# PSUM banks in a two-layer hybrid block: five for the projections and three for the mixers, in place of six and two

## The chip, the cores and the metric

The kernel runs on one core of one Trainium2 chip. The metric is the device time of one execution in microseconds (us). A core has a matrix engine, TensorE (PE in the profile, with its weight loader shown apart as PEld), a vector engine (DVE), a scalar engine (ACT), a general engine (POOL) and a queue that issues transfers (SP). Matmuls write into PSUM, which here is eight banks of 128 partitions by 512 fp32 values; the other engines read the results from there.

## The reference, cut to what matters

Two layers over 1024 tokens and a model width of 2048. Each layer normalises and modulates the input, projects it with one wide matrix, sends the parts of the projection through three mixers, gates them, and projects back:

```python
def hybrid_layer(x, c, positions, ...):
    shift, scale, gate = jnp.split(jax.nn.silu(c) @ w_mod + b_mod, 3, axis=-1)
    h = rms_norm(x, g_pre) * (1.0 + scale[:, None, :]) + shift[:, None, :]
    proj = h @ w_in
    a_q, a_k, a_v, s_u, s_v, c_q, c_k, c_v, c_g, z = jnp.split(proj, offsets, axis=-1)
    a_q, a_k = partial_rope(a_q, positions), partial_rope(a_k, positions)
    y_a = sliding_window_attention(a_q, a_k, a_v, swa_sinks)         # 16 heads, 4 kv heads, window 128
    y_b = chunked_spatial_gating(gelu(s_u), gelu(s_v), sg_w, sg_b, sg_ln_g, sg_ln_b)
    log_alpha = log_sigmoid(c_g @ gla_w_gate_up + gla_b_gate) / 16.0
    y_c = rms_norm(gated_linear_attention(c_q, c_k, c_v, log_alpha), gla_norm_g)
    y = jnp.concatenate([y_a, y_b, y_c], axis=-1) * jax.nn.silu(z)
    return x + gate[:, None, :] * rms_norm(y @ w_out, g_post)

def reference(x, c, positions, w_mod, ...):
    for l in range(2):
        x = hybrid_layer(x, c, positions, w_mod[l], ...)
    return x
```

## The kernel before, in words

The tokens are split into two halves of 512, and a layer runs over one half after the other, so there are four phases (l, h). A phase has an input part (`in_phase`) and an output part (`out_phase`).

**Projections.** Both parts are made of groups. A group (`group`, L394) computes 512 columns by 512 tokens as four results of 128x512, each in a PSUM bank of its own; one group of 256 columns (`ck`) uses two banks. It loops over the 2048 rows of the weight in eight chunks of two k of 128. For each k and each result m it issues three matmuls (fp32 split into a high and a low part: L381 to L383 where the weight is stationary, L389 to L391 where the activations are). `w_take` hands it a split chunk: L367 on ACT makes the high part, L368 on DVE the low one. The whole kernel has 11,904 such projection matmuls. The groups of an input part come in this order: keys and gla queries (`kcq`), gla keys (`ck`), values, `q0`, `cv`, `q1`, and then `zc`, `sv`, `su`, `zb`, `za0`, `za1`.

**Evacuation.** When its last k is done, a group's four banks are read, and the next group can use a bank once its reader has ended. The reader depends on the group: `evac` is an ACT copy (L768, or L770 with a scale); `silu2` a tanh on ACT and a product on DVE (L427, L428); in the output part ACT takes the sum of squares (L993) and DVE the product with the gate (L995). `gelu2`, used for `sv` and `su`, copies the bank first (L435, ACT) and then works on two tiles of the pool `t2`: square (L436, ACT), L437 and L438 (DVE), tanh (L439, ACT), and the last product (L440, DVE). `t2` has four tiles, so two results are in work at a time.

**Mixers.** Beside the projections run lanes: generators for attention (`att`), gated linear attention (`gla`), spatial gating (`sg`), the modulation (`mod`) and the end of an output part (`fin`). After every three matmuls of a group `tick()` lets a lane go on when its delay has passed, so mixer matmuls stand between projection matmuls in the program. Their results go into the second PSUM pool by `mxt()`. The ones that matter here: attention scores (L491) take two banks at a time and are read by L498 or L500 (ACT) and L501 (DVE); the transposes of the probabilities (L533) wait for their normalisation (L520) and are read by L536; the gla score blocks (L634, L650, L656) are read by `put` (L621, DVE, eight small copies); the transposes of the next phase's input (`h_fill`, L287) by L289. L263 is the sum of squares of the second half's input rows (`x_stats`), L224 a step of the modulation.

**What sets the order.** The program names work in the order above; a planner in the framework then sets the order on each engine from the program's order, priorities (`urgent()` lifts by 300, `evac` by 600) and the pools: an instruction that needs a tile is placed when the planner sees the tile free. The sizes of the two PSUM pools therefore set both which bank a group waits for and the order of instructions on the engines.

The first group, in the start of the kernel, has six results; its banks are taken at once at L1060:

```python
        psk = [pjt() for _ in range(6)]
```

Of the kernel before, what the change touches and what calls it, by code (L numbers as in the profile page):

```python
# [18 lines left out]
PSUM = bass.MemoryType.PSUM  # L19
# [20 lines left out]
def hybrid_kernel(ctx: ExitStack, tc: tile.TileContext, a, y_out):  # L40
# [6 lines left out]
    whl_p = ctx.enter_context(tc.tile_pool(name="whl", bufs=3))  # L47
    t2_p = ctx.enter_context(tc.tile_pool(name="t2", bufs=4))
    sm = ctx.enter_context(tc.tile_pool(name="sm", bufs=2))
    pj = ctx.enter_context(tc.tile_pool(name="pj", bufs=6, space=PSUM))  # L50
    mx = ctx.enter_context(tc.tile_pool(name="mx", bufs=2, space=PSUM))
    pools = {}

    V, S, G, PE = nc.vector, nc.scalar, nc.gpsimd, nc.tensor
# [1 line left out]
    def load(out, in_):  # L56
        nc.sync.dma_start(out=out, in_=in_)

    def urgent():
        return tc.high_priority(offset=PRIO)  # L60
# [35 lines left out]
    def t2(shape=(P, 512), dt=F32):  # L96
        return t2_p.tile(list(shape), dt, tag="t2", name="t2")
# [7 lines left out]
    def mxt():  # L105
        return mx.tile([P, 512], F32, tag="mx", name="mx")

    def pjt():
        return pj.tile([P, 512], F32, tag="pj", name="pj")
# [13 lines left out]
    def rsqrt(out, src, n, pool=sm):  # L123

        i = pool.tile([P, n], I32, tag="rq_i", name="rq_i")
        V.tensor_scalar(i, src.bitcast(I32), 1, None, ALU.logical_shift_right)
        V.tensor_scalar(i, i, -1.0, 1597463007.0, ALU.mult, ALU.add)
        yv = i.bitcast(F32)
        for it in range(3):
            w = pool.tile([P, n], F32, tag="rq_w", name="rq_w")  # L130
            V.tensor_tensor(w, yv, yv, ALU.mult)
            V.scalar_tensor_tensor(w, w, -0.5, src, ALU.mult, ALU.mult)
            dst = out if it == 2 else yv
            V.scalar_tensor_tensor(dst, w, 1.5, yv, ALU.add, ALU.mult)
            yv = dst
# [51 lines left out]
    def mod_columns(l, c, acc, partials):  # L187

        tp = mxt()
        if partials == P:  # L190
            for s in range(4):
                PE.matmul(tp[:, s:s + 1], lhsT=acc[:, s * P:(s + 1) * P], rhs=ones[:, 0:1], start=True, stop=True)
            m = tp[:, 0:4]
        else:
            for s in range(4):
                PE.transpose(tp[:, s * P:(s + 1) * P], acc[:, s * P:(s + 1) * P], ident)
            m = col(4, "mod_m")
            V.tensor_reduce(m, tp.rearrange("p (s r i) -> p s r i", s=4, i=32)[:, :, :, 0], AX.X, ALU.add)
        m = m.rearrange("p (k s) -> p k s", k=2)
        j = slice(2 * c, 2 * c + 2)  # L200
        V.tensor_tensor(bcol[l][:, j], m[:, :, 0], mb[l][:, 0, j], ALU.add)
        t = col(2, "mod_t")
        V.tensor_tensor(t, m[:, :, 1], mb[l][:, 1, j], ALU.add)
        V.scalar_tensor_tensor(acol[l][:, j], t, 1.0, gpc[l][:, j], ALU.add, ALU.mult)
# [147 lines left out]
    def w_load():  # L352
        if wat[0] < len(wsrc):
            src, cols = wsrc[wat[0]]
            wat[0] += 1
            if deep and wat[0] % 2:
                raw = pools["pt"].tile([P, KC, cols], F32, tag="PT", name="wraw2")
            else:
                raw = wraw_p.tile([P, KC, cols], F32, tag="wraw", name="wraw")
            load(raw, src)  # L360
            raws.append(raw)

    def w_split():
        if raws:
            raw = raws.popleft()
            hl = whl_p.tile([P, 2] + list(raw.shape[1:]), F32R, tag="whl", name="whl")
            S.copy(hl[:, 0], raw)  # L367
            V.tensor_tensor(hl[:, 1], raw, hl[:, 0].bitcast(F32), ALU.subtract)  # L368
            ready.append(hl)
            w_load()  # L370
# [6 lines left out]
    def mm_f(ps, hl, k2, m, slot, k):  # L377

        c = slice(m * P, (m + 1) * P)
        whi, wlo = hl[:, 0, k2, c], hl[:, 1, k2, c]  # L380
        PE.matmul(ps, lhsT=whi, rhs=slot[:, 0], start=(k == 0), stop=False)  # L381
        PE.matmul(ps, lhsT=whi, rhs=slot[:, 1], start=False, stop=False)  # L382
        PE.matmul(ps, lhsT=wlo, rhs=slot[:, 0], start=False, stop=(k == NK - 1))  # L383
# [630 lines left out]
    with tc.tile_pool(name="start", bufs=1) as st:  # L1014

        load(mb[0], a["b_mod_col"][0])
        load(gpc[0], a["g_pre"][0])
        xq = [act_p.tile([P, 2, H], F32, tag="act", name="xq") for _ in range(8)]
        for c in range(8):
            load(xq[c], a["x_f"][0, 2 * c:2 * c + 2].rearrange("j p t -> p j t"))  # L1020
        scb = st.tile([P, NK, 32], F32, name="scb")
        V.tensor_copy(scb, sc.unsqueeze(2).broadcast_to([P, NK, 32]))
        ws, raw_q, hl_q = deque(), deque(), deque()

        def first_load(k):
            if k < NK:
                r = wraw_p.tile([P, 1, 768], F32, tag="wraw", name="wraw")
                load(r[:, 0, 0:512], a["w_in"][0, 0, :, k])
                load(r[:, 0, 512:], a["w_ck"][0, :, k])
                raw_q.append(r)  # L1030

        def first_split():
            r = raw_q.popleft()
            hl = whl_p.tile([P, 2, 1, 768], F32R, tag="whl", name="whl")
            S.copy(hl[:, 0], r)  # L1035
            V.tensor_tensor(hl[:, 1], r, hl[:, 0].bitcast(F32), ALU.subtract)
            hl_q.append(hl)

        def mod_load(c, part):
            if c < 8:  # L1040
                w = st.tile([P, 8, 512], F32, name="wm0", bufs=3)
                load(w, a["w_mod"][0, c, :, 8 * part:8 * part + 8])
                ws.append(w)
        mod_load(0, 0)
        mod_load(0, 1)
        mod_load(1, 0)
        first_load(0)


        sums = mxt()  # L1050
        for c in range(8):
            sq = st.tile([P, 2, H], F32, name="sq", bufs=2)
            S.activation(sq, xq[c], AF.Square)
            s2 = st.tile([P, H], F32, name="s2", bufs=2)
            V.tensor_tensor(s2, sq[:, 0], sq[:, 1], ALU.add)
            PE.matmul(sums, lhsT=ones, rhs=s2, start=(c == 0), stop=(c == 7))
        r0 = st.tile([P, H], F32, name="r0")
        V.tensor_scalar(r0, sums, 1.0 / D, EPS, ALU.mult, ALU.add)
        rsqrt(r0, r0, H, st)
        psk = [pjt() for _ in range(6)]  # L1060

        def project(k):
            first_split()
            if k >= NK - 2:
                w_load()
            hl = hl_q.popleft()
            for m in range(6):
                mm_f(psk[m], hl, 0, m, slots[k], k)

        def mod_products(mps, part):  # L1070

            w = ws.popleft()
            for kk in range(8):
                k = 8 * part + kk
                r = 32 * (k % 4)
                PE.matmul(mps[r:r + 32, :], lhsT=scb[:, k], rhs=w[:, kk], start=(k < 4), stop=(k >= 12))  # L1076

        def fill(c, mps):
            acc = st.tile([P, 512], F32, name="mod_acc", bufs=2)
            S.copy(acc, mps)  # L1080
            mod_columns(0, c, acc, 4)
            for j in range(2):
                k = 2 * c + j
                xt, b = t2(), bcol[0][:, k:k + 1]
                V.scalar_tensor_tensor(xt, xq[c][:, j], acol[0][:, k:k + 1], r0, ALU.mult, ALU.mult)
                s = act_p.tile([P, 2, 512], F32R, tag="act", name="act")
                S.activation(s[:, 0], xt, AF.Identity, bias=b)
                V.scalar_tensor_tensor(s[:, 1], xt, b, s[:, 0].bitcast(F32), ALU.add, ALU.subtract)
                slots.append(s)

        for c in range(8):
            if c:
                mod_load(c, 1)
                first_load(2 * c - 1)
            mps = mxt()
            mod_products(mps, 0)
            if c:
                project(2 * c - 2)  # L1100
                mod_load(c + 1, 0)
                first_load(2 * c)
            mod_products(mps, 1)
            with urgent():
                fill(c, mps)
            if c:
                project(2 * c - 1)
            if c == 5:
                for _ in rope_tables(0):
                    pass  # L1110
        first_load(NK - 1)
        project(NK - 2)
        project(NK - 1)
        w_split()
        w_split()
# [147 lines left out]
```

## Time and profile before

| | |
|---|---|
| median of 3 runs | 3080.06 us (3077.67 to 3081.16) |
| profiled execution | 3080.16 us |
| its span | 3078.4 us |
| mean granted TensorE clock | 0.993 |
| TensorE busy | 3005.8 us, 98% |
| weight loader busy | 2445.1 us, 79% |
| DVE busy | 1840.0 us, 60% |
| ACT busy | 1198.9 us, 39% |
| DMA, mean | 152 GB/s |

The span is the time from the first to the last instruction of the profiled execution. Its own time is 1.8 us longer and is the one to compare with the runs. A row of the timeline gives the start and the length of an instruction, and in brackets how long its engine sat idle before it and what ended that. Matmuls overlap: a bar is longer than the distance from one start to the next.

### The profile page before, as it was taken

Reading aid. Unit: us, or ns where it says so; the run is one execution under the profiler, and the core shown is the slowest. Engines: PE = TensorE matmul, PEld = TensorE weight load, DVE = VectorE, ACT = ScalarE, POOL = GpSimd, SP = SyncE. Lnnn points to the kernel's source line nnn. Section 1 sums busy time; section 2 is a strip of 40 time slices with the busy share of each in tenths; the row PEclk is TensorE's granted clock in tenths of the full one; section 3 lists DMA queues with packets and bytes.
Section 4 is the critical chain, followed back from the end, with each engine's and each line's share of the span. In section 5 each row is a group of like instructions: output and inputs, shape, how many; then the busy total and the mean of one; then the engine's idle time right before and its main releaser. Section 6 shows DMA issues by size and latency. Waiting matters only on the chain.

```text
span 3078.4 us, 44118 instructions
## 1 busy us (share of the span) xinstructions
PE 3005.8 (98%) x17298; PEld 2445.1 (79%) x17298; DVE 1840.0 (60%) x2956; ACT 1198.9 (39%) x2367; POOL 24.9 (1%) x68
## 2 busy tenths in 40 slices
PE   7999999999998999999999999999999999999998
PEld 4678777888887887888888887888888888788886
DVE  4678777563867877744364766644346476663425
ACT  3355345232434544323244544423233444342323
POOL 0000000000000000000000000000000000000000
PEclk9999999999999999999999999999999999999999
DMA  9745457575775445644455223334446322343535
GB/s 393 260 138 154 141 171 219 156 232 161 236 226 161 124 131 175 184 130 137 120 168 154 86 72 99 114 118 143 117 129 192 102 80 84 111 131 106 167 103 168
DMA packets 216448, 468.96 MB, mean 152 GB/s; under 512 B 21008, under 2 KB 74672, under 8 KB 214192
## 3 DMA queue, kind: packets, MB, share of 16 engines
q1 hardware_dynamic: 216240, 466.15, 48.9%
q8 instruction: 135, 2.21, 0.3%
q14 instruction: 73, 0.60, 0.1%
HBM read 429.37 MB, written 36.70 MB: 151 GB/s over the span
## 4 chain that ended last, share of the span: by engine, by line
PE 81%; DMA 7%; DVE 7%; ACT 3%; issue 2%; SPq 0%; DVEq 0%; ACTq 0%
PE pj L381 13%; PE pj L382 12%; PE pj L383 12%; PE pj L389 12%; PE pj L391 12%; PE pj L390 12%; DMA wm<-in_w_mod_dram 4%; PE mx L491 2%; PE mx L547 1%; DVE whl L368 1%; DMA t<-in_gla_norm_g_dram 1%; DVE ma L224 1%; DMA wm<-in_x_dram 1%; PE mx L1076 1%; PE mx L533 1%
## 5 line engine op out<-in xcount | busy, mean ns | idle before, releaser
L368 DVE TENSOR_TENSOR whl<-wraw,whl 128x1024 fp32r<-128x1024 f32 (+2 forms) x504 | 587.2, 1165 | 706.1 <-ACT whl L367 705.2
L367 ACT CAST whl<-wraw 128x1024 fp32r<-128x1024 f32 (+2 forms) x504 | 506.0, 1004 | 1128.1 <-PE pj L391 576.1
L389 PE MATMUL pj<-whl,act 128*128 128x512 f32 (+1 forms) x2048 | 784.1, 383 | 0.0
L390 PE MATMUL pj<-whl,act 128*128 128x512 f32 (+1 forms) x2048 | 776.8, 379 | 0.0
L391 PE MATMUL pj<-whl,act 128*128 128x512 f32 (+1 forms) x2048 | 776.6, 379 | 0.0
L381 PE MATMUL pj<-act,whl 128*128 128x512 f32 x1920 | 763.4, 398 | 9.3 <-ACT whl L1035 3.6
L383 PE MATMUL pj<-act,whl 128*128 128x512 f32 x1920 | 749.2, 391 | 3.7 <-DVE whl L368 3.7
L382 PE MATMUL pj<-act,whl 128*128 128x512 f32 x1920 | 751.5, 391 | 0.0
L381 PEld LDWEIGHTS pj<-act,whl 128*128 128x128 f32 x1920 | 361.5, 188 | 109.3 <-issue 23.0
L391 PEld LDWEIGHTS pj<-whl,act 128*128 128x128 f32 x2048 | 385.7, 188 | 72.4 <-issue 0.7
L389 PEld LDWEIGHTS pj<-whl,act 128*128 128x128 f32 x2048 | 386.2, 189 | 69.2 <-issue 2.1
L390 PEld LDWEIGHTS pj<-whl,act 128*128 128x128 f32 x2048 | 386.1, 189 | 67.4 <-issue 1.2
L383 PEld LDWEIGHTS pj<-act,whl 128*128 128x128 f32 x1920 | 361.9, 188 | 82.1 <-DVE whl L368 5.0
L382 PEld LDWEIGHTS pj<-act,whl 128*128 128x128 f32 x1920 | 362.1, 189 | 71.7 <-issue 1.1
L224 DVE SCALAR_TENSOR_TENSOR ma<-wm,sc,ma 128x512 f32<-128x512 f32 x240 | 179.5, 748 | 117.0 <-DMA wm<-in_w_mod_dram 115.3
L517 ACT ACTIVATE M<-M,at_nm 128x128 f32<-128x128 f32 x256 | 99.7, 391 | 50.0 <-DVE at_nm L509 50.0
L536 DVE TENSOR_TENSOR PT<-mx,amask 128x1024 f32<-128x1024 f32 x64 | 77.3, 1218 | 15.7 <-PE mx L533 15.5
L501 DVE COPY_PREDICATED M<-pmask,mx 128x256 f32<-128x256 uint8 x128 | 50.6, 441 | 54.4 <-ACT M L500 42.9
L491 PE MATMUL mx<-kh,qs 128*128 128x256 f32 (+1 forms) x256 | 67.7, 297 | 7.7 <-DVE hold L621 7.5
L491 PE MATMUL mx<-kl,qs 128*128 128x256 f32 (+1 forms) x256 | 66.1, 286 | 0.0
L547 PEld LDWEIGHTS mx<-PT,v 128*64 128x64 f32 x960 | 53.1, 137 | 15.1 <-issue 7.1
L500 ACT COPY M<-mx 128x256 f32<-128x256 f32 x96 | 31.7, 374 | 84.9 <-PE mx L491 84.8
(224 smaller groups left out, 2331.7 us busy)
## 6 DMA issues: line engine op xcount, KB each, us to landing
wraw<-in_w_in_dram SPq DMA_DIRECT2D x312, 512.0 KB, 3.6
wraw<-in_w_out_dram SPq DMA_DIRECT2D x136, 512.0 KB, 3.6
wm<-in_w_mod_dram SPq DMA_DIRECT2D x256, 256.0 KB, 3.3
wm<-in_w_mod_dram SPq DMA_DIRECT2D x16, 2048.0 KB, 13.5
y<-at SPq DMA_DIRECT2D x64, 256.0 KB, 2.8
q<-y SPq DMA_DIRECT2D x64, 256.0 KB, 3.3
q<-x SPq DMA_DIRECT2D x36, 256.0 KB, 2.7
wraw<-in_w_vcg_dram SPq DMA_DIRECT2D x32, 272.0 KB, 2.9
```

What stands on the lines that cost most here:

```text
L224: V.scalar_tensor_tensor(acc, ws[k], sc[:, k:k + 1], acc, ALU.mult, ALU.add)
L367: S.copy(hl[:, 0], raw)
L368: V.tensor_tensor(hl[:, 1], raw, hl[:, 0].bitcast(F32), ALU.subtract)
L381: PE.matmul(ps, lhsT=whi, rhs=slot[:, 0], start=(k == 0), stop=False)
L382: PE.matmul(ps, lhsT=whi, rhs=slot[:, 1], start=False, stop=False)
L383: PE.matmul(ps, lhsT=wlo, rhs=slot[:, 0], start=False, stop=(k == NK - 1))
L389: PE.matmul(ps, lhsT=slot[:, 0, c], rhs=whi, start=(k == 0), stop=False)
L390: PE.matmul(ps, lhsT=slot[:, 0, c], rhs=wlo, start=False, stop=False)
L391: PE.matmul(ps, lhsT=slot[:, 1, c], rhs=whi, start=False, stop=(k == NK - 1))
L491: PE.matmul(sps[p][:, b, k0:], lhsT=qs[:, p, n * P:(n + 1) * P], rhs=keys[2 * j + p][:, n * P + k0:n * P + 256], start=(part == 0), stop=( ...
L517: S.activation(Mf[:, k], Mf[:, k], AF.Exp, bias=nm[:, k:k + 1], scale=0.125, accum_out=den[:, k:k + 1])
L547: PE.matmul(yp[64 * p:64 * p + 64, n * P:(n + 1) * P], lhsT=vv[:, g * 64:g * 64 + 64], rhs=pts[p][:, w, n], start=(w == 0), stop=(w == 1 o ...
```

## The change

Pool `pj`, from which the groups take their banks, has five in place of six, and pool `mx`, from which the mixers take theirs, three in place of two; the sum stays eight. The first group takes one of its six banks from `mx`.

```diff
-    pj = ctx.enter_context(tc.tile_pool(name="pj", bufs=6, space=PSUM))
-    mx = ctx.enter_context(tc.tile_pool(name="mx", bufs=2, space=PSUM))
+    pj = ctx.enter_context(tc.tile_pool(name="pj", bufs=5, space=PSUM))
+    mx = ctx.enter_context(tc.tile_pool(name="mx", bufs=3, space=PSUM))
...
-        psk = [pjt() for _ in range(6)]
+        psk = [mxt()] + [pjt() for _ in range(5)]
```

The change moves instructions. The first place is TensorE at the change from group `su` to group `zb` in the second phase (1274 us in the trace before). pj_11271 to pj_11274 are the four banks of the new group, m=0 to m=3; act_6759 is the activation of its k=0, act_6780 that of k=1. Before:

```order
L382 MATMUL pj_11273<-act_6759,whl_11168 128x512
L383 MATMUL pj_11273<-act_6759,whl_11168 128x512
L381 MATMUL pj_11274<-act_6759,whl_11168 128x512
L382 MATMUL pj_11274<-act_6759,whl_11168 128x512
L383 MATMUL pj_11274<-act_6759,whl_11168 128x512
L381 MATMUL pj_11271<-act_6780,whl_11168 128x512
L382 MATMUL pj_11271<-act_6780,whl_11168 128x512
```

And in the changed kernel at the same place:

```order
L383 MATMUL pj_11273<-act_6759,whl_11168 128x512
L381 MATMUL pj_11271<-act_6780,whl_11168 128x512
L382 MATMUL pj_11271<-act_6780,whl_11168 128x512
L383 MATMUL pj_11271<-act_6780,whl_11168 128x512
L381 MATMUL pj_11272<-act_6780,whl_11168 128x512
L382 MATMUL pj_11272<-act_6780,whl_11168 128x512
L383 MATMUL pj_11272<-act_6780,whl_11168 128x512
L381 MATMUL pj_11273<-act_6780,whl_11168 128x512
L382 MATMUL pj_11273<-act_6780,whl_11168 128x512
L383 MATMUL pj_11273<-act_6780,whl_11168 128x512
L381 MATMUL pj_11274<-act_6759,whl_11168 128x512
```

The three matmuls of m=3 for k=0 now stand behind the nine of m=0 to m=2 for k=1. The same holds at the other changes of group behind a gelu.

The second place is ACT at the gelu near 501 us. pj_4233 and pj_4234 are the first two banks that are read; the rows of L263 belong to the sum of squares of the input rows. Before:

```order
L263 ACTIVATE junk_4885,xss_4499<-wm_4883 128x128
L263 ACTIVATE junk_4887,xss_4499<-wm_4883 128x128
L263 ACTIVATE junk_4889,xss_4499<-wm_4883 128x128
L263 ACTIVATE junk_4891,xss_4499<-wm_4883 128x128
L263 ACTIVATE junk_4912,xss_4499<-wm_4910 128x128
L263 ACTIVATE junk_4914,xss_4499<-wm_4910 128x128
L435 COPY t2_4661<-pj_4233 128x512
L263 ACTIVATE junk_4916,xss_4499<-wm_4910 128x128
L436 ACTIVATE t2_4662<-t2_4661 128x512
L435 COPY t2_4670<-pj_4234 128x512
```

In the changed kernel:

```order
L263 ACTIVATE junk_4885,xss_4499<-wm_4883 128x128
L263 ACTIVATE junk_4887,xss_4499<-wm_4883 128x128
L435 COPY t2_4661<-pj_4233 128x512
L263 ACTIVATE junk_4889,xss_4499<-wm_4883 128x128
L436 ACTIVATE t2_4662<-t2_4661 128x512
L435 COPY t2_4670<-pj_4234 128x512
L263 ACTIVATE junk_4891,xss_4499<-wm_4883 128x128
L367 CAST whl_4700<-wraw_4565 128x1024
```

Four of the six L263 ahead of the first copy now stand behind it, three of them between the second copy and the third.

The third place is TensorE near 371 us, where the transposes of the probabilities (L533) stand between projection matmuls. mx_3465 and mx_3484 are two mixer banks; act_639 and act_644 are the activations of two successive k. Before:

```order
L389 MATMUL pj_3252<-whl_3361,act_639 128x512
L390 MATMUL pj_3252<-whl_3361,act_639 128x512
L391 MATMUL pj_3252<-whl_3361,act_639 128x512
L389 MATMUL pj_3249<-whl_3361,act_644 128x512
L390 MATMUL pj_3249<-whl_3361,act_644 128x512
L391 MATMUL pj_3249<-whl_3361,act_644 128x512
L389 MATMUL pj_3250<-whl_3361,act_644 128x512
L390 MATMUL pj_3250<-whl_3361,act_644 128x512
L391 MATMUL pj_3250<-whl_3361,act_644 128x512
L533 MATMUL mx_3465<-ident_81,M_3315 128x128 x4
L533 MATMUL mx_3484<-ident_81,M_3315 128x128 x4
```

In the changed kernel:

```order
L389 MATMUL pj_3252<-whl_3361,act_639 128x512
L533 MATMUL mx_3465<-ident_81,M_3315 128x128 x4
L390 MATMUL pj_3252<-whl_3361,act_639 128x512
L391 MATMUL pj_3252<-whl_3361,act_639 128x512
L533 MATMUL mx_3484<-ident_81,M_3315 128x128 x4
L389 MATMUL pj_3249<-whl_3361,act_644 128x512
```

The first four transposes stand eight projection matmuls earlier, the second four six.

## Rows read from the trace of the kernel before

**Rows 1.** The page's busy shares: microseconds, share of the span, instructions

```profile
PE 3005.8 (98%) x17298; PEld 2445.1 (79%) x17298; DVE 1840.0 (60%) x2956; ACT 1198.9 (39%) x2367; POOL 24.9 (1%) x68
```

**Rows 2.** Timeline near 1592: start, length, engine line operation, [idle before <-releaser]

```profile
1591.69 2.15 DVE L995 TENSOR_TENSOR hold<-pj,gp 128x512 f32<-128x512 f32 x3
1592.81 0.39 PE L381 MATMUL pj<-act,whl 128*128 128x512 f32 x1
1593.49 0.39 PE L381 MATMUL pj<-act,whl 128*128 128x512 f32 x1
```

**Rows 3.** Tile view, mixer tiles: TensorE idle (us, times) until the named one

```profile
  DVE hold L621: 9.1, 4
  DVE PT L536: 2.7, 3
```

**Rows 4.** Waits of the weight loader: us in total, times, longest

```profile
PEld mx L491 <- issue: 9.9, 8, 6.6
PEld mx L634 <- issue: 5.0, 10, 1.9
PEld mx L491 <- DVE M L501: 3.1, 10, 0.5
PEld mx L634 <- DVE PT L536: 2.1, 3, 1.3
```

**Rows 5.** Timeline near 991: gla copies and the next scores

```profile
989.45 2.03 DVE L621 COPY_PREDICATED hold<-gmask,mx 32x128 f32<-32x128 uint8 x8
991.41 0.55 PE L491 MATMUL mx<-kh,qs 128*128 128x256 f32 x1 [6.18 <-DVE hold L621]
```

**Rows 6.** Timeline near 1274: gelu, the next group's matmuls

```profile
1273.90 0.39 PE L381 MATMUL pj<-act,whl 128*128 128x512 f32 x1
1279.99 0.59 ACT L435 COPY t<-pj 128x512 f32<-128x512 f32 x1 [1.11 <-DVE hold L440]
```

**Rows 7.** Timeline near 453: gelu of the first phase

```profile
453.27 0.39 PE L381 MATMUL pj<-act,whl 128*128 128x512 f32 x1
458.04 0.60 PE L533 MATMUL mx<-ident,M 128*128 128x128 f32 x4
458.21 0.59 ACT L435 COPY t<-pj 128x512 f32<-128x512 f32 x1
```

**Rows 8.** Timeline near 1967: gelu in layer 2

```profile
1967.38 0.39 PE L381 MATMUL pj<-act,whl 128*128 128x512 f32 x1
1971.39 0.59 ACT L435 COPY t<-pj 128x512 f32<-128x512 f32 x1 [1.11 <-DVE hold L440]
```

**Rows 9.** Timeline near 501: gelu behind the row statistics

```profile
504.07 0.31 ACT L263 ACTIVATE junk<-wm 128x128 bf16<-128x128 f32 x1
504.38 0.57 ACT L435 COPY t<-pj 128x512 f32<-128x512 f32 x1
505.00 0.79 PE L381 MATMUL pj<-act,whl 128*128 128x512 f32 x1 [2.91 <-ACT t L435]
510.18 0.58 ACT L435 COPY t<-pj 128x512 f32<-128x512 f32 x1 [0.24 <-DVE hold L440]
```

**Rows 10.** Timeline near 867: the group of two banks

```profile
867.62 0.39 PE L381 MATMUL pj<-act,whl 128*128 128x512 f32 x1
870.78 1.05 ACT L768 COPY t<-pj 128x512 f32<-128x512 f32 x2
873.37 0.50 PE L381 MATMUL pj<-act,whl 128*128 128x512 f32 x1 [0.83 <-ACT whl L367]
875.73 0.50 PE L383 MATMUL pj<-act,whl 128*128 128x512 f32 x1 [1.62 <-DVE whl L368]
```

**Rows 11.** Timeline near 821: group behind an output group

```profile
823.65 0.50 PE L381 MATMUL pj<-act,whl 128*128 128x512 f32 x1 [1.32 <-DVE hold L995]
```

**Rows 12.** Timeline near 371: transposes of the probabilities

```profile
371.04 1.07 PE L533 MATMUL mx<-ident,M 128*128 128x128 f32 x8 [0.44 <-DVE M L520]
```

**Rows 13.** Windows near 504: us, PE, PEld, DVE, ACT, POOL, clock, DMA, GB/s

```profile
504.10:510.90 6.80, 5.90 (x14) 4.47 (x15) 4.48 (x10) 6.50 (x15) 0.00 (x0) 0.50 0.64 189
```

## The prediction

> **What bounds the kernel now.** I read the page's busy shares first, then how far apart matmuls start, then who keeps TensorE waiting, once for the mixers' tiles and once for the weight loader, and last the stretches around each change of projection group. TensorE is busy for 98% of the span [rows 1], and DVE (60%) and ACT (39%) have room. So the end is set by how many matmuls TensorE has to start and by the gaps between starts; DVE or ACT matter only where TensorE waits for them. The 98% hides small gaps, because a bar lasts 0.39 us while the starts at 1592.81 and 1593.49, three matmuls apart, give 0.227 us each [rows 2]. A gap shorter than 0.16 us therefore never shows as idle, and every printed wait is 0.16 us short.
>
> The Trainium skill, "Perfetto Trace Analysis", section "Identifying the Most-Contended Engine", says that the busy share of matmuls is a poor measure of the room left, and that the loader's share is a better one. The trace bears it out: 98% against 79% [rows 1]. By that rule the gains below would be read from the loader alone, 13.5 us instead of my 11, and the sum would end at 3079.7 instead of 3082.
>
> No matmul is added or removed, so the change can work only through waits: those of mixers for a mixer bank, which a third bank can shorten, and those of projection groups for a projection bank, which five instead of six can lengthen.
>
> **What the third mixer bank gives.** A mixer matmul that waits for a bank waits for the reader of an earlier mixer tile. For the mixers' tiles TensorE sat idle 9.1 us for L621 (the copies into the gla state tiles) and 2.7 us for L536 (the probabilities after their transpose) [rows 3]. Of the 9.1, one wait of 6.18 us stays: the scores at 991.41 take two banks at once, and the L621 copies that hold two banks start only at 989.45, because DVE works through other lines before [rows 5]. With three banks one is free there, but two are needed. That leaves 2.9 + 2.7 = 5.6 us as the lower bound.
>
> The loader shows more, since its idle time is not shortened by long bars: L491 behind the score readers L501 3.1 us, L634 behind L536 2.1 us, and without a named releaser 9.9 − 6.6 = 3.3 us for L491 and 5.0 us for L634 [rows 4]. The sum, 13.5 us, is the upper bound. I take the 5.2 us with a named reader in full, and 70% of the other 8.3, because these name none: **11 us gained**, nearer to the loader's rows, which measure starts.
>
> The order of instructions adds little: 322 of 3217 mixer matmul instructions stand earlier on TensorE, mostly by 1 to 8 projection matmuls.
>
> **What the sixth projection bank gave.** A group of four takes four banks while the group before is still being read out. With six banks its m=2 is the first to need a bank of the group before (the reader of m=0); with five it is m=1, and m=3 now needs the third reader. Each bank is thus wanted three matmuls earlier, 0.68 us. At an ordinary change of group this is covered: the L995 products that free the banks start at 1591.69, the three take 2.15 us, and the first bank, free near 1592.4, is wanted at 1593.49 after the change [rows 2]. That leaves 1.1 us, so I cost most changes of group at nothing. The others, one by one:
>
> - *Gelu at 1274.* gelu2 copies each bank into a t2 tile, two tiles per m, out of four. The third copy therefore waits for the first L440, and ends at 1279.99 + 0.59 = 1280.58 [rows 6]. The order shows nine matmuls of k=1 put ahead of m=3, which move its first matmul 2.04 us back. It falls 18 matmuls behind the one at 1273.90, at 1273.90 + 18 × 0.227 = 1277.98. With 0.05 us to start, as the 505.00 against 504.95 of [rows 9] shows, the new wait is **2.65 us**.
> - *Gelu at 453.* The third copy ends at 458.21 + 0.59 = 458.80; m=3 is due at 453.27 + 18 × 0.227 = 457.36, and the four transposes of the row at 458.04, which come before it and last 0.60 us with the last bar run out (0.33 us by starts, my estimate), make it 457.69 [rows 7]: **1.1 us**.
> - *Four gelu changes in layer 2*, all like the one at 1967: the copy ends at 1971.39 + 0.59 = 1971.98, m=3 is due at 1967.38 + 18 × 0.227 + 0.33 = 1971.80 [rows 8]; with the start 0.25 us each, **1.0 us**. Without the 0.33 us it would be more, with an earlier L440 nothing.
> - *Gelu at 501.* Now m=2 waits 2.91 us, really 3.07, for the first copy, which ends at 504.38 + 0.57 = 504.95 behind six L263 [rows 9]. In the new order four of these stand behind it, 0.31 us each, so the copy ends some 1.2 us earlier. But m=1 wants it 0.68 us earlier: wait 2.5 us. The third copy ended 510.18 + 0.58 − 504.95 = 5.8 us behind the first, after 0.24 us without work [rows 9]; three L263 now fill that and add 0.7, so 6.5. Between the two TensorE has 15 matmuls, 3.4 us at 0.227: a second wait of 3.1. Together 5.6 against 3.07: **2.5 us**, between −1.1 (at the slow clock of rival A the 15 matmuls last 6.5 us and cover the third copy, and the first comes 1.7 us earlier) and 3.8 (the first no earlier).
> - *Gelu at 1225*, the eighth, has its copies among mixer work. I take the smallest wait of the other early ones, **1.1 us**, between 0 and 2.65.
> - *The group of two banks at 867.* It finds one bank free and needs for the second the first L768 copy, half way through a row of two that starts at 870.78: ready near 871.3. It is due at 867.62 [rows 10]: wait 3.75 us. But the same group already waits for its weight splits at 873.37 (0.83) and 875.73 (1.62), really 2.8 us with the hidden 0.16 each, and a later start lets these go: **1.0 us**.
> - *821.* The wait for L995 (1.32 us) [rows 11] comes one bank earlier: at most 0.68 us, **0.7 us**.
> - *Other changes of group with less cover than 0.68 us*: seven, of which each could lose that much less its cover; I take **1.5 us**, between 0 and 3.4 (five in full).
> - *Mixers moved onto data that is not ready.* At 371 the transposes already wait 0.44 us for L520 [rows 12], and the order puts them eight projection matmuls earlier, 1.8 us: **1.5 us**, between 0 and 1.8.
>
> The losses sum to 13 us. At the least there remain 2.65 + 1.1 + 1.0 + 0.7 − 1.1 = 4.35; at the most 2.65 + 1.1 + 1.0 + 3.8 + 2.65 + 1.0 + 0.7 + 3.4 + 1.8 = 18.1.
>
> The first group's borrowed bank costs nothing: it leaves two for the mixers at the start, as before, and its matmuls keep their order.
>
> **Sum.** 13 − 11 = +2 us on the profiled execution's own 3080.16 us, 0.1 above the median of the runs (3080.06): 3082.
>
> **Rivals.**
>
> *A, the clock: slower.* After the wait of 2.91 us the stretch 504.10 to 510.90 ran at a granted clock of 0.50, the lower of the two levels, 1.2 GHz; its 14 matmuls, 3.2 us at 0.227 each, took the 5.9 us from 505.00 on [rows 9, 13]. Each such fall thus cost 2.7 us beyond the wait. If the new waits at 867, 1274 and 371 and the second one at 501 bring a further fall each, three or four of them cost 8 to 11 us on top of the forecast's +2: 3090 to 3093, about 3092. It decides from two further falls on (5.4 us). For it: 867 and 1274 would wait as long as 501 did. Against it: the stretches after 867 hold waits today. The Trainium skill, "TensorE: Matmul & The Clock Gate", section "A second HAM failure mode: psum-queue depth-cycling", tells of a kernel that cycled through PSUM banks, in which small idle times of TensorE between groups made the clock go up and down and cost throughput. By that page fewer projection banks would hurt beyond their waits. In the trace the clock falls behind a long wait, the one of 2.91 us, and over the whole span the granted clock is 0.993.
>
> *B, the loader is right: faster.* Gains of 13.5 us against the least losses of 4.35: −9.15, 3071. For it: the earlier mixer matmuls also free DVE and ACT earlier, and many losses stand on covers worked out to tenths. Against it: the wait at 1274 follows from the t2 tiles and would be hard to miss.
>
> *C, the cover fails: much slower.* If the nine matmuls ahead of m=3 hide nothing (because m=1 or m=2 already waits until the third copy ends), all eight gelu changes lose 2.04 us more: 2 + 16.3, 3098. The order speaks against it, since m=0 to m=2 go first.
>
> *D, hardly anything happens:* nine tenths of the mixer matmuls keep their place, and gains and losses both stay small. The result is the forecast's.
>
> **How the numbers follow.** Forecast with D 0.60, A 0.19, B 0.15, C 0.06. The forecast's own ends are 4.35 − 11 = −6.65 and 18.1 − 11 = +7.1, so 3073.5 to 3087.3. Upwards the range takes in A, to 3093; downwards it stops at 3073, which leaves out most of B, and C: under 0.2. A difference of 0.2% (6.2 us) is about what a measurement of this kernel can tell: B is faster by more, A and C slower, the rest within.
>
> **What would show it.** In the changed profile: a wait of 2 to 3 us for L435 near 1274 at m=3 of the next group, and one near 867 for L768 of 3 to 4 us with the waits for L367 and L368 behind it gone; two waits instead of one near 501; idle time for L621 near 6 us instead of 9, the long one near 991 still there; loader waits for L501 and L536 gone. TensorE's total idle time for L435 would rise by 5 us or more. The prediction is wrong if the granted clock is 0.50 in new stretches, if waits for banks turn up at ordinary changes of group (where I count 1.1 us of cover), or if the idle time for mixer tiles stays what it is.

## The result, and the profile after

The changed kernel takes 3087.47 us (median of 20 runs, 3079.44 to 3093.64), the kernel before 3079.80 us (20 runs, 3076.40 to 3084.57). The ratio is 1.0023, with a 95% interval from 1.0016 to 1.0029: about 7 us slower, between 5 and 9. The forecast was 3082 us, with 0.60 on a difference within 0.2%; the time lies in the range (3073 to 3093), and the slowdown of 0.23% (0.16% to 0.29%) cannot be told from 0.2%. The profiled execution has a span of 3088.8 us, 10.4 more than before, so it lies a few us above the median.

First the busy shares of the changed kernel, from its page, against [rows 1]:

```profile
PE 3008.9 (97%) x17298; PEld 2447.4 (79%) x17298; DVE 1841.3 (60%) x2956; ACT 1199.1 (39%) x2367; POOL 24.8 (1%) x68
```

The same work in a span that is 10 us longer. Who TensorE waited for in the changed kernel (us in total, times, longest):

```profile
PE pj L381 <- ACT t L435: 7.3, 5, 2.7
PE mx L491 <- DVE hold L621: 5.4, 3, 2.0
PE mx L491 <- DVE qs L471: 3.9, 1, 3.9
PE pj L381 <- ACT t L768: 3.4, 1, 3.4
PE pj L381 <- DVE hold L995: 2.6, 1, 2.6
PE mx L634 <- DVE hold L621: 2.1, 1, 2.1
```

Two groups stand out. The waits for a projection bank (L435, L768, L995) have grown: L435 from 3.5 us, L995 from 1.3 us [rows 11], L768 from nothing. For L621, 9.1 us before [rows 3], there are 7.5 us by these two rows, and a new wait for L471 of 3.9: where L621 and L536 had cost 11.8 us, L621 and L471 now cost 11.4. The loader's rows that answer to [rows 4]:

```profile
PEld mx L491 <- issue: 11.5, 8, 4.3
PEld mx L634 <- issue: 6.8, 14, 2.2
PEld mx L491 <- DVE M L501: 1.5, 2, 1.1
```

The row for L536 is gone, as forecast; the one for L501 is halved, where the forecast had it gone too. The unnamed ones have grown, from 14.9 to 18.3 us.

To see where the time went I paired the 11,904 projection matmuls of the two traces by their rank in time and took the change of the distance between them over each stretch. At the changes of group that the prediction named:

| near (us before) | forecast | paired starts |
|---|---|---|
| 453, gelu | +1.1 | +0.9 |
| 501, gelu | +2.5 | −2.2 |
| 821, L995 | +0.7 | +1.2 |
| 867, two banks | +1.0 | +4.3 − 3.6 = +0.7 |
| 1225, gelu | +1.1 | +1.0 − 0.4 = +0.6 |
| 1274, gelu | +2.65 | +4.6 |
| four gelus of layer 2 | +1.0 | +1.6 |

Together 7.4 us, against 10.05 forecast. The rest of the 10.4 us lies in stretches with mixers: +1.9 near 250, +2.1 near 340, −1.1 near 410, −3.1 near 920, +2.3 from 966 to 996, +3.5 near 1020, −1.4 near 1045, and smaller ones. There the forecast had a gain of 11 us.

Two places of the changed kernel in full. At the gelu change near 1274 (1286 now), the timeline:

```profile
1284.87 0.58 ACT L435 COPY t<-pj 128x512 f32<-128x512 f32 x1 [1.11 <-DVE hold L440]
1285.51 0.50 PE L381 MATMUL pj<-act,whl 128*128 128x512 f32 x1 [2.66 <-ACT t L435]
1286.85 0.63 PE L383 MATMUL pj<-act,whl 128*128 128x512 f32 x1
1287.28 0.63 PE L381 MATMUL pj<-act,whl 128*128 128x512 f32 x1
```

and the windows around it, with those behind the waits at 501 and 867 (us, then busy of PE, PEld, DVE, ACT, POOL, granted clock, DMA share, GB/s):

```profile
503.50:510.00 6.50, 3.62 (x15) 2.36 (x14) 4.42 (x8) 6.41 (x18) 0.00 (x0) 1.00 0.54 156
510.00:516.00 6.00, 6.00 (x28) 4.95 (x27) 5.83 (x15) 3.56 (x6) 0.00 (x0) 1.00 0.50 145
873.00:878.00 5.00, 5.00 (x16) 3.93 (x15) 4.70 (x14) 1.94 (x4) 0.00 (x0) 0.66 0.61 198
1286.00:1290.00 4.00, 4.00 (x13) 3.08 (x12) 3.92 (x8) 3.32 (x6) 0.00 (x0) 0.58 0.69 239
```

The wait is the forecast one, 2.66 us. Behind it comes what rival A described: matmuls start 0.43 us apart and the granted clock is 0.58 in that window, so part of it at the lower level, 1.2 GHz. Near 501 the opposite happened: the clock is 1.00, where it was 0.50 before [rows 13].

The long wait that I expected to stay, near 991 [rows 5], stands in the changed kernel in two pieces:

```profile
986.96 0.55 PE L491 MATMUL mx<-kh,qs 128*128 128x256 f32 x1 [3.90 <-DVE qs L471]
992.71 0.55 PE L491 MATMUL mx<-kh,qs 128*128 128x256 f32 x1 [2.00 <-DVE hold L621]
```

The window of the first piece, in the same columns:

```profile
982.70:990.00 7.30, 3.40 (x11) 2.67 (x10) 7.21 (x11) 2.65 (x4) 0.00 (x0) 0.75 0.26 73
```

and of the whole wait in the kernel before:

```profile
984.80:991.40 6.60, 0.43 (x2) 0.02 (x1) 6.43 (x14) 1.14 (x2) 0.00 (x0) 0.80 0.51 151
```

DVE is busy 7.21 of 7.30 us and 6.43 of 6.60. TensorE waits for DVE's work there, and the third bank changed little more than which of DVE's instructions the wait is named after. That DVE's load sets the length of this wait is argued from these shares; no run here changes that load alone.

### The profile page after: what moved, and what is told of

It reads as the page before. It is cut to its first block, busy times and chain, and to the rows that moved or that the text cites. A ratio compares the mean times of both kernels' runs of the same rounds, so it can differ in the third digit from the quotient of the medians.

```text
span 3088.8 us, 44124 instructions
## 1 busy us (share of the span) xinstructions
PE 3008.9 (97%) x17298; PEld 2447.4 (79%) x17298; DVE 1841.3 (60%) x2956; ACT 1199.1 (39%) x2367; POOL 24.8 (1%) x68
## 4 chain that ended last, share of the span: by engine, by line
PE 78%; DMA 8%; DVE 8%; ACT 3%; issue 2%; SPq 0%; DVEq 0%; ACTq 0%
PE pj L381 12%; PE pj L383 12%; PE pj L382 12%; PE pj L389 11%; PE pj L391 11%; PE pj L390 11%; DMA wm<-in_w_mod_dram 5%; PE mx L491 2%; DVE whl L368 2%; PE mx L547 1%; DVE ma L224 1%; DMA t<-in_gla_norm_g_dram 1%; ACT whl L367 1%; ACT M L517 1%; PE mx L533 1%
## 5 line engine op out<-in xcount | busy, mean ns | idle before, releaser
L368 DVE TENSOR_TENSOR whl<-wraw,whl 128x1024 fp32r<-128x1024 f32 (+2 forms) x504 | 587.8, 1166 | 721.3 <-ACT whl L367 716.6
L224 DVE SCALAR_TENSOR_TENSOR ma<-wm,sc,ma 128x512 f32<-128x512 f32 x240 | 180.2, 751 | 115.0 <-DMA wm<-in_w_mod_dram 113.4
L536 DVE TENSOR_TENSOR PT<-mx,amask 128x1024 f32<-128x1024 f32 x64 | 77.3, 1221 | 15.7 <-PE mx L533 15.5
L501 DVE COPY_PREDICATED M<-pmask,mx 128x256 f32<-128x256 uint8 x128 | 50.7, 442 | 52.7 <-ACT M L500 42.8
L491 PEld LDWEIGHTS mx<-kh,qs 128*128 128x128 f32 x256 | 51.7, 202 | 16.7 <-issue 11.5
```

The costliest lines, as they stand in the source:

```text
L224: V.scalar_tensor_tensor(acc, ws[k], sc[:, k:k + 1], acc, ALU.mult, ALU.add)
L491: PE.matmul(sps[p][:, b, k0:], lhsT=qs[:, p, n * P:(n + 1) * P], rhs=keys[2 * j + p][:, n * P + k0:n * P + 256], start=(part == 0), stop=( ...
L536: V.tensor_tensor(pt, tp.rearrange("p (n q) -> p n q", n=NT).unsqueeze(1).broadcast_to([P, 2, NT, P]), amask.unsqueeze(2).broadcast_to([P, ...
```

## The experiments

Twelve further kernels, all timed against the kernel before. The ratios, with 95% intervals:

| banks | other edit | median us | ratio |
|---|---|---|---|
| 6 and 2 | none (before) | about 3080 | 1 |
| 5 and 3 | none (the change) | 3087.47 | 1.0023 [1.0016, 1.0029] |
| 5 and 2, one idle | none | 3087.38 | 1.0018 [1.0008, 1.0028] |
| 4 and 4 | none | 3085.67 | 1.0012 [1.0004, 1.0021] |
| 6 and 2 | gelu2 | 3077.95 | 0.9988 [0.9979, 0.9997] |
| 5 and 3 | gelu2 | 3081.59 | 1.0002 [0.9994, 1.0011] |
| 4 and 4 | gelu2 | 3080.55 | 1.0001 [0.9992, 1.0009] |
| 6 and 2 | wm | 3070.57 | 0.9969 [0.9957, 0.9981] |
| 5 and 3 | wm | 3081.65 | 1.0003 [0.9992, 1.0014] |
| 6 and 2 | gelu2, wm | 3069.81 | 0.9962 [0.9950, 0.9975] |
| 5 and 3 | gelu2, wm | 3070.08 | 0.9967 [0.9955, 0.9979] |
| 4 and 4 | gelu2, wm | 3066.03 | 0.9953 [0.9940, 0.9966] |
| 5 and 2 | fillers | 3090.73 | 1.0027 [1.0016, 1.0037] |
| 5 and 3 | L420 on GpSimd | 3100.89 | 1.0061 [1.0047, 1.0076] |

**One half of the change alone: five and two.** On the changed kernel:

```diff
+    mx = ctx.enter_context(tc.tile_pool(name="mx", bufs=2, space=PSUM))
+    px = ctx.enter_context(tc.tile_pool(name="px", bufs=1, space=PSUM))
...
+        psk = [px.tile([P, 512], F32, tag="px", name="px")] + [pjt() for _ in range(5)]
```

> Five banks for the projections, two for the mixers; the eighth bank serves only the first group and is idle afterwards. Theory 1 (the sixth projection bank is what is missed, and the third mixer bank gives some of it back): slower than the changed kernel by what the third bank gave, 3 to 11 us, so 3090 us or more, with the waits of the changed kernel for L435 at 1274 (2.7 us) and for L768 at 867 (3.4 us) still there. Theory 2 (the third mixer bank itself costs, because mixer matmuls move forward onto data that is not ready): faster than the changed kernel, about 3084 us, with the projections' waits alone left.

The time is that of the changed kernel. The third mixer bank is therefore worth 1.0018 − 1.0023 = −0.0005, give or take 0.0012: between 2 us gained and 5 us lost, not 11 gained. And to do without the sixth projection bank costs 0.0018, 2 to 9 us, not 13. Neither theory is right as written: the loss is the projections', as theory 1 says, but the third bank gives back nothing that can be measured; that it costs a few us, as theory 2 says, is not excluded. The waits of this kernel:

```profile
PE pj L381 <- ACT t L435: 7.6, 5, 2.5
PE mx L491 <- DVE hold L621: 6.0, 3, 4.7
PE pj L381 <- DVE hold L995: 3.3, 1, 3.3
```

The wait for L768 near 867, expected to be still there, has all but gone (0.3 us), so the traces of the two kernels differ in more than the mixers' waits. Near 991 TensorE waits 4.65 us in one piece, less than with the third mixer bank.

**The gelu copy made independent of the t2 tiles**, on five and three and on six and two:

```diff
     def gelu2(dst, ps):
-        x = t2()
         u = t2()
         with urgent():
-            S.copy(x, ps)
-        S.activation(u, x, AF.Square)
+            S.copy(dst, ps)
+        S.activation(u, dst, AF.Square)
...
-        V.scalar_tensor_tensor(dst, u, 1.0, x, ALU.add, ALU.mult)
+        V.scalar_tensor_tensor(dst, u, 1.0, dst, ALU.add, ALU.mult)
```

> The changed kernel with gelu2 copying the bank into its own result tile instead of a t2 tile, so that it takes one t2 tile per result and the third copy waits for no L440. Theory 1: the waits for L435 go (7.3 us by the page) and with them the fall of the clock behind 1274: 8 to 11 us faster than the changed kernel, 3077 to 3080 us. Theory 2: half of that at most, 3083 us or more, because the mixers' moves remain.

> The kernel before with the same gelu2. Theory 1: with six banks the third copy is never late, so nothing changes beyond 501: 3078 to 3082 us. If the t2 tiles cost something by themselves whatever the number of banks, it gains as much as the changed kernel does by the same edit (8 us or more: 3072 us or less).

On five and three it gives 0.0021, about 6.5 us, between the two forecasts (8 to 11 us, or half of that at most): the waits for L435 are gone, but a new one stands near 550:

```profile
PE pj L381 <- DVE t L428: 4.3, 1, 4.3
PE pj L381 <- ACT hold L434: 1.5, 1, 1.5
```

DVE shows why, in the timeline of the same kernel: it stood in L224 until a transfer came, and the L428 that frees the bank was queued behind it.

```profile
546.64 0.75 DVE L224 SCALAR_TENSOR_TENSOR ma<-wm,sc,ma 128x512 f32<-128x512 f32 x1 [3.44 <-DMA wm<-in_w_mod_dram]
549.11 1.28 DVE L428 SCALAR_TENSOR_TENSOR t<-t,pj 128x512 f32<-128x512 f32 x2
```

On six and two it gives 0.0012 (0.0003 to 0.0021), a gain I had not expected: near 501 the wait for the copy is 1.35 us in place of 2.91 there, and the slow stretch behind it is gone (a granted clock of 1.00 from 503 to 510; −4.2 us by paired starts).

**Four and four.** The sizes of the pools, and two borrowed banks for the first group.

```diff
+    pj = ctx.enter_context(tc.tile_pool(name="pj", bufs=4, space=PSUM))
+    mx = ctx.enter_context(tc.tile_pool(name="mx", bufs=4, space=PSUM))
...
+        psk = [mxt() for _ in range(2)] + [pjt() for _ in range(4)]
```

> Four banks for the projections, four for the mixers (the first group borrows two). Theory 1: every change of group wants its banks another 0.68 us earlier: the ordinary ones still have 0.4 us of cover, the eight gelu changes lose about 2 us each and the short ones 0.7 each: 3100 to 3110 us. Theory 2: as little again as from two to three mixer banks, 3085 to 3095 us.

Theory 1's 3100 us or more did not come: 3085.67 us, in theory 2's range. The waits of this kernel:

```profile
PE pj L381 <- ACT t L435: 6.7, 5, 2.9
PE mx L491 <- DVE qs L471: 3.6, 1, 3.6
PE pj L381 <- ACT t L768: 2.1, 1, 2.1
PE pj L381 <- DVE hold L995: 2.0, 1, 2.0
```

The waits for L435 are no longer than with five banks, and L621 is no longer among TensorE's waits in this trace. Near 991 one wait of 3.64 us is left, where the third bank had left 5.90. So it is the fourth mixer bank that shortens the waits for L621; two banks under the L621 copies and two for the scores make four.

> Four banks for the projections, four for the mixers, with the gelu2 that needs one t2 tile. The first four runs gave: five and two 1.0018 of before, five and three with this gelu2 1.0002, six and two with it 0.9988, four and four 1.0012. Theory 1 in its new form (each split of the banks loses at the gelu copies, and a fourth mixer bank, not the third, takes away the waits for L621): the gelu edit gives 4 to 7 us here as well, so 0.999 of before, 3076 to 3080 us. If the fourth mixer bank gains nothing and four and four was only quicker by chance, it stands no better than five and three with the same edit: 3081 us or more.

3080.55 us, level with five and three with the same edit (1.0001 against 1.0002) and between the two forecasts. Near 550 this kernel loses 7.4 us to the kernel before by paired starts (five and three with the same edit 6.2): TensorE waits 4.4 us there for L428, as in the rows above. And a wait for L621, 2.02 us near 990, is back, so the fourth bank does not end these waits in every order.

**Fillers into the waits**, on five and two: matmuls into the idle bank, 12 ahead of m=1 near 825 and 9 ahead of m=3 near 1283.

```diff
+    def warm(hl, slot, n):
+        if n:
+            wt = px.tile([P, 512], F32, tag="px", name="px")
+            for _ in range(n):
+                PE.matmul(wt, lhsT=hl[:, 0, 0, 0:P], rhs=slot[:, 0], start=True, stop=True)
...
+                    if k == 0:
+                        warm(hl, slots[0], fill.get(m, 0))
                     mm(ps[m], hl, k2, w, slots[k], k)
```

> Five and two (the eighth bank idle) with filler matmuls into the idle bank: 12 where the wait of 3.46 us for L995 stands near 825, 9 where the wait of 2.70 us for L435 stands near 1283; their results are read by nobody. Each is shorter than the wait it stands in (2.7 and 2.0 us at 0.227 each). If the idle time of TensorE itself brings the lower clock behind it, the stretches at a granted clock of 0.50 behind both places go while the end of each wait stays: 2 to 4 us faster than five and two, 3083 to 3085 us. If the clock falls for another reason, the stretches stay and so does the time, 3087 us, or it rises by up to 5 us where the fillers do not fit into the wait.

The windows behind the two waits, five and two without fillers:

```profile
829.00:836.00 7.00, 7.00 (x19) 5.52 (x20) 6.55 (x20) 0.00 (x0) 0.00 (x0) 0.58 0.50 154
1286.00:1290.00 4.00, 4.00 (x12) 3.20 (x13) 3.26 (x6) 2.75 (x5) 0.00 (x0) 0.65 0.74 239
```

and with them:

```profile
829.00:836.00 7.00, 7.00 (x33) 5.79 (x32) 6.51 (x19) 1.87 (x5) 0.00 (x0) 1.00 0.51 158
1286.00:1290.00 4.00, 3.77 (x17) 3.13 (x18) 3.92 (x8) 2.89 (x6) 0.00 (x0) 1.00 0.80 245
```

With TensorE at work during the wait the clock stays at 1.00 behind both places. The second is the cleaner test: the bank comes free at nearly the same time (1286.22 for 1285.95), and the nine fillers leave 1.19 us idle in place of 2.54. There the idle time brings the fall. At the first place DVE's L995 also started 1.77 us sooner (826.45 for 828.22), so that the wait would have been shorter without fillers too; the 3.6 us that paired starts show as saved there hold both. But the time did not get shorter (1.0027 against 1.0018, the intervals overlap). Paired starts show the saving gone again by 890 (+3.9 near 880, where TensorE now waits 0.95 us for an ACT copy and 1.98 us for L368) and another 3.3 us lost near 990, where the wait for L621 (the line is L629 in this kernel) is longer:

```profile
996.69 0.55 PE L499 MATMUL mx<-kh,qs 128*128 128x256 f32 x1 [7.13 <-DVE hold L629]
```

It was 4.65 us without the fillers: TensorE begins to wait 0.7 us sooner and the copies come 1.8 us later. DVE is busy 7.53 us of the 7.7 from 989.0 to 996.7, so a lead that TensorE wins ahead of this stretch is no gain. Why DVE comes later here stays open.

**DVE's load in that stretch**, on the changed kernel: one product of `rope` on GpSimd.

```diff
-        V.tensor_tensor(dst, raw, cst[0], ALU.mult)
+        G.tensor_tensor(dst, raw, cst[0], ALU.mult)
```

> The changed kernel with one of rope's four steps (L420, 0.69 us on DVE, 40 times) on GpSimd. In the stretch 982.7 to 990 DVE is busy 7.21 of 7.30 us while TensorE waits for L471 and then L621. If the third mixer bank gave nothing because DVE bounds that stretch, the two waits together (3.9 + 2.0 us) get shorter by 0.7 to 1.4 us and the time by 1 to 3 us: 3084 to 3086 us. If a bank is what is waited for, nothing changes (3087 us); if GpSimd is so slow that its product comes after DVE's, it gets slower (3090 us).

Slower than the changed kernel by some 12 us, so this does not test what it was for. The product takes 1.6 us on GpSimd, and the chain to L471 got longer:

```profile
L420 POOL TENSOR_TENSOR q<-q,cs 128x512 f32<-128x512 f32 x32 | 52.2, 1636 | 858.6 <-DVE at L419 823.3 <-ACT at L551 35.3
```

```profile
PE mx L491 <- DVE qs L471: 7.5, 4, 4.1
PE mx L491 <- DVE hold L621: 6.7, 3, 2.8
```

What it does show is that the scores wait for this chain: with the same banks and a longer chain, TensorE waits for L471 at four places in place of one (7.5 us for 3.9). The waits for L621 are no longer than before in all (6.7 us for 7.5). Near 991 the two waits come to 4.14 and 1.63 us, 5.8 in all for 5.9, and DVE is still busy 7.94 us of the 8.00 from 984 to 992.

**A third buffer for the modulation's weights** (pool `wm`, 2 to 3), which are what DVE's L224 waits for. The input rows that L263 reads on ACT take their tiles from the same pool. The edit is made with and without the new gelu2, and on each split.

```diff
-    ... ("wm", 2) ...
+    ... ("wm", 3) ...
```

> The kernel before with the new gelu2 and three buffers for the modulation's weights in place of two. With the new gelu2 alone DVE stood in L224 until a transfer of these weights came, and the first L428 near 550 was 1.9 us late. If that transfer is late for want of a buffer, the wait goes: 2 us faster than with the new gelu2 alone, 3075 to 3077 us. If the transfers are late because of their bandwidth or their queue, no change: 3078 us.

> The kernel before with three buffers for the modulation's weights alone. If these two edits add up, it gains what the third buffer gave on top of the new gelu2, 0.0026: 3071 to 3074 us. If the third buffer only mended a wait that the new gelu2 had opened at 550, it gains nothing: 3079 to 3081 us.

> The changed kernel with three buffers for the modulation's weights alone. If the loss of the change is at the gelu copies and at changes of group, it stays, 5 to 8 us behind the kernel before with the same third buffer. If the loss came from mixers that move onto late transfers, the third buffer mends it and the two are level.

> The changed kernel (five and three banks) with the new gelu2 and three buffers for the modulation's weights; six and two with both came to 0.9962 of before. If the banks cost only through the gelu copies and DVE's waits for those weights, this stands within 0.0005 of six and two: 3069 to 3072 us. If the shortage of projection banks costs at the other changes of group too (821, 867), it stays 3 to 6 us behind: 3073 to 3077 us.

> Four and four banks with both edits. If the fourth mixer bank takes away the waits for L621 (7.5 us before) and its loss at the projections is the one seen so far, it is level with six and two with both edits, 3068 to 3072 us. If the loss at the projections weighs more once the other waits are gone, 3074 us or more.

The buffer is the largest single gain of the study: 0.0031 on the kernel before, some 9.5 us, more than any split of the banks moved the kernel without other edits (0.0023). DVE's waits for the transfers, kernel before:

```profile
DVE ma L224 <- DMA wm<-in_w_mod_dram: 115.3, 83, 4.7
```

and with the third buffer:

```profile
DVE ma L224 <- DMA wm<-in_w_mod_dram: 59.0, 53, 4.0
```

Half of DVE's idle time in L224 goes. Paired starts show where these two traces part: 5.4 us near 501, 1.7 near 821 and 2.3 near 870. Near 501 it is not L224: the rows of L263 have ended by 482.7 us, well before the first gelu copy at 496.0, and the wait of [rows 9] and the slow stretch of [rows 13] are gone. At 821 the wait for L995 [rows 11] is gone. How the gain divides between L224 and L263 is not shown. The guess that the buffer only mended 550 was wrong: it gains by itself, and six and two with both edits came to 3069.81 us where 3075 to 3077 was expected. Together the two edits give 0.0038, where 0.0012 and 0.0031 make 0.0043; the difference is within the noise, though both edits act on the wait near 501.

With these kernels the cost of the change, five and three against six and two, is known four times: 0.0023 (neither edit), 0.0034 (wm), 0.0014 (gelu2), 0.0005 (both). With the old gelu2 that is 0.0028 on average, 9 us; with the new one 0.0010, 3 us; each good to about 0.001. By these averages some two thirds of the loss hang on the gelu copies, and what is left may be nothing. With both edits five and three came to the 3069 to 3072 us of the first forecast. The third buffer alone does not mend the loss: five and three stays 11 us behind six and two (5 to 8 were expected), so late transfers through this pool are not its cause. In that pair of traces five and three loses 2.5 us at the gelu near 453 and 5.1 us at the one near 501.

The best kernel is four and four with both edits: 3066.03 us, 14 us under the kernel before. Without wm this split was no faster than the kernel before (with wm alone it was not run). It is faster than the 3068 to 3072 expected. Its waits for L621 have come down to one of 0.7 us, the ones for the gelu copy (L434 in this kernel) to 2.1 us, and the largest left in the projections is 3.2 us:

```profile
PE pj L381 <- ACT v L768: 3.2, 2, 2.1
PE pj L381 <- ACT hold L434: 2.1, 2, 1.7
PE mx L491 <- DVE qs L471: 1.3, 2, 1.0
PE mx L491 <- DVE hold L621: 0.7, 1, 0.7
```

By paired starts it gains 5.5 us on the kernel before from 960 to 1000, around the long wait of [rows 5], where six and two with both edits loses 1.9. Against six and two with both edits (0.9962) the intervals of the times overlap, so that four and four is the better split is likely but not shown.

## Why the prediction was right and wrong

The time fell into the range, but partly by luck. The sum +2 came from two terms that were both too large, 13 us of losses for about 5.5 and 11 us of gains for about none, and their errors had opposite signs. The forecast's own ends reached to 3087.3, and the measured 3087.47 lies at that edge; the range holds it because room was left for rival A, to 3093. Of the three signs of being wrong that the prediction named, two turned up: a granted clock of 0.50 in a new stretch (1024 to 1026 us), and idle time for mixer tiles that stayed what it was (11.8 us for L621 and L536, then 11.4 for L621 and L471). Of the third, waits at ordinary changes of group, there is one, 0.59 us near 337.

- **"11 us gained" by the third mixer bank: wrong, and the step that failed.** Measured: between −5 and +2 us. I read the waits of [rows 3, 4] as waits for a bank, because their releaser reads one. More than half of the 11 us, 5.8, I took from loader rows that name no releaser at all [rows 4], and these grew from 14.9 to 18.3 us. The traces show that at the largest place the releaser's engine is full: with a bank more TensorE goes on to the next thing that DVE owes it (L471 for L621). I had that one wait of 6.18 us stay, by the count of banks, and did not ask of the others whether DVE was full there. The Trainium skill, "Perfetto Trace Analysis", section "Optimization Strategy", says that repeated gaps on the engine that should be full can mean too few PSUM buffers; here, at the longest gap, one buffer more changed the name and hardly the length (6.18 us before, 3.90 + 2.00 after), and the measurement decides; with two more it was 3.64 us, so the page is not refuted. Near 250 the planner used the third bank to move half of the scores forward, and TensorE then stood 1.73 us for L621 between the two halves, where it stood 0.74 before.
- **"Losses 13 us": right in kind, too large.** Measured with five and two: 2 to 9 us. The waits at single places came nearly as worked out: 1274 2.66 us for 2.65, 867 3.36 idle (3.5 by starts) for 3.75 with the later waits gone as forecast (0.7 net for 1.0), 453 0.9 for 1.1, 821 1.2 for 0.7. The four gelus of layer 2 cost 1.6 for 1.0.
- **501: wrong sign.** The second wait came (2.55 us idle for 3.1 forecast); of the first, forecast at 2.5, there was next to nothing, and 0.33 us for the second copy in its place. The first copy ended 1.95 us sooner (503.00 for 504.95), and TensorE came 1.6 us later because of waits ahead of it, which I had not counted. The sum is near the old wait, but the slow stretch of [rows 13] did not follow; why a wait of 2.55 us brought none is not shown. My own lower bound had a part of this.
- **371: 1.5 us forecast, none came.** The transposes wait 0.42 us for L520, as before; L520 had come forward with them.
- **Rival A, the clock: half right.** Behind 867 and 1274 the clock fell, and near 1020 a stretch at 0.52 followed a wait at L650 that no release explains (2.1 us, 0.8 before). One fall, near 501, went away. The fillers show the cause of such a fall near 1283, not its share in the 7 us. The Trainium skill, "TensorE: Matmul & The Clock Gate", section "A second HAM failure mode: psum-queue depth-cycling", has small idle times between groups that make the clock go up and down. In these traces it was single long waits, 2.66 us at 1274, that a fall followed, and no run here shows it for the ordinary changes of group.
- **Rival B** needed the 13.5 us that did not come; that 98% against 79% bears out the loader's rows, as the prediction says, does not follow from two shares, and those rows forecast even more of what did not come. **Rival C** did not come: the nine matmuls did their cover. **Rival D** was right in that most of the program kept its time, wrong in the size.
- The wait at L650 near 1020 names no releaser, but the traces hint at one. It ends 1.46 us after a 16 KB transfer of the instruction queue has landed, and 1.45 us after one in the kernel before; that transfer starts at 1021.53 us in place of 1019.92. In all fourteen traces, each of the 35 unnamed waits of TensorE over 0.3 us (the start of the kernel left out) ends 1.2 to 1.6 us after such a landing. So TensorE most likely waits there for its own instructions. No run tests this.
- What stays open: why the fourth mixer bank shortens the wait near 991 where the third did not, why that transfer comes later in the changed kernel, and how much of the loss each fall of the clock carries over many runs, since each trace is one execution. What theory 1 made of another 0.68 us per bank, 3100 us or more, is refuted by four and four, and nothing was put in its place.

## What to carry to other kernels

A wait for a bank's reader is a wait for a bank only if the reader's engine has time to spare there: look at its busy share in the very window of the wait before counting a buffer as a gain. Here a third bank changed little with DVE full, and a fourth shortened the wait, so the share is a warning and not a proof. Do not count idle time that names no releaser as a wait for the thing you are about to add. Where an evacuation borrows a scratch tile, the scratch pool sets when the bank comes free; copying into the result's own tile was worth about as much as a bank (0.0012 and 0.0021, against 0.0018). And look at what an in-order engine stands in while others queue behind it: one more input buffer for side jobs of DVE and ACT gained more than any split of the banks.

## What the runs showed of the hardware

- An idle TensorE can bring the lower clock, and work of no use prevents it: with 12 and 9 filler matmuls in waits of 3.46 and 2.70 us (3.30 and 2.54 as printed) the granted clock stayed at 1.00 where it had been 0.58 and 0.65 on average behind them; at the first of the two places the wait itself had become shorter. Not every wait is followed by a fall: behind 2.55 us near 509 it stayed 1.00.
- Waits of TensorE for which the trace names no releaser ended 1.2 to 1.6 us after a transfer of the instruction queue had landed, in 35 of 35 cases over the fourteen traces.
- A product of two 128x512 fp32 tiles takes 1.6 us on GpSimd where DVE takes 0.69 us.
